# Fewer weight pieces split ahead, the first attention's rotation on VectorE alone, and two state-space operations moved to VectorE

## The chip, the cores and the metric

The kernel runs on one core of one Trainium2 chip. What counts is the device time of one execution in microseconds (us). Each version is timed in several runs; the median is compared.

## The reference, cut to what matters

Two blocks of two layers each, on one sequence of 256 tokens of width 1024, all in float32. The first block has a short convolution mixer, then a dilated-window attention with three groups of eight heads, each layer followed by a squared-ReLU MLP and a gated per-layer projection. The second block has SwiGLU layers around a state-space mixer, and an attention that shares keys and values. The attention of the first block rotates the first 32 of the 128 rows of each query and key head:

```python
def partial_rotary(x, positions):
    ...
    x1 = xf[..., :half]
    x2 = xf[..., half:ROPE_DIM]
    out = jnp.concatenate([x1 * cos - x2 * sin, x2 * cos + x1 * sin, xf[..., ROPE_DIM:]], axis=-1)
```

The state-space mixer is a linear recurrence over the sequence with complex coefficients, written as an associative scan:

```python
    _, _, x_re, x_im = lax.associative_scan(combine, (la_re, la_im, bu_re, bu_im), axis=1)
```

## The kernel before

Activations stay in SBUF, transposed: 128 rows of the width by 256 tokens. Weights come from memory in pieces of 128x2048 float32 values (1 MB), in one fixed order, PLAN. To keep float32 accuracy each weight piece and each activation is split into a rounded part and a rest: ScalarE copies a half piece of 128x1024 into whi (L289), VectorE subtracts it from the raw piece into wlo (L290). Three matmuls then make one product: high by high, high by low, low by high (mm3, L362 to L364). One piece is 48 matmuls.

Three pieces of raw weights, and three of whi and wlo, fit into the ring of buffers. piece() hands out the split piece that is due. On the way it calls fetch(), which splits up to three pieces ahead (ahead=3) and loads up to six ahead. split() is the loop that does so; split_open() takes the buffers, split_half() issues the two instructions for a half piece.

A norm needs the sum of squares of the new activations before its factor R is known. The matmuls of the next phase start without it; its evacuations (rotate, evac, gate) are put on the list "late" by when_scaled() and issued once norm_bc() has made R. In piece(), a fetch that comes in the second piece of such a phase goes on the same list, if two pieces are split ahead:

```python
        if 0 < len(self.todo) < 4 and self.n_split >= i + 2:

            self.late.append(lambda: self.behind(fetch))
        else:
            fetch()
```

behind() ties its instructions to follow the last ones traced on each engine. Background work (tables and weights of the state-space mixer, built during the MLPs; keys and values later) advances by steps, each tied to follow in the same way.

The order on each engine is fixed when the kernel is compiled (TCARGS, L208): a scheduler walks through the program on a modelled time line, gives each engine the earliest instruction in program order that is ready, and lets later work go ahead where an engine would idle. The order of the first attention's pieces is written out by hand (ATT_SEQ, L60). On the chip each engine runs its list in order.

In the first attention, qk() makes one query and one key head of one group in an accumulator, and rotate() scales by R, shuffles the first 32 rows, multiplies by sine and cosine and adds, on POOL (L764 to L767), then splits the result into qh and ql. head() does scores, softmax, transposes and the product with the values. In s5(), chain(q) runs the recurrence of a quarter of the channels: two products, an add, a scan, two products, a difference.

Of the kernel before, what the change touches and what calls it, by code (L numbers as in the profile page):

```python
# [10 lines left out]
F32 = mybir.dt.float32  # L11
# [3 lines left out]
OP = mybir.AluOpType  # L15
# [3 lines left out]
S = 256  # L19
# [113 lines left out]
PLAN = plan()  # L133
# [89 lines left out]
class Ker:  # L223
# [17 lines left out]
    def load(self, i):  # L241
        nc = self.nc
        while self.n_load < min(i, len(PLAN)):
# [22 lines left out]
            self.raw[n] = t  # L266
            self.n_load += 1

    def split(self, i):
        while self.n_split < min(i, len(PLAN)):  # L270
            todo = self.split_open(1)
            for c in range(2):
                self.split_half(todo, c)
# [467 lines left out]
    def attention_(self, x):  # L741
        nc, at = self.nc, self.pp
# [7 lines left out]
        swap = [(i + 16) % 32 for i in range(32)]  # L750
        bc = lambda t: t[:, None, :].to_broadcast([32, 2, S])
        V, QK = {}, {}

        def qk(h, g):
            acc = self.cols(x, "attn_w_qkv", 0, (g * D + h * 128, A + g * D + h * 128),
                            ps="big" if (h, g) == (1, 0) else "acc")
            self.when_scaled(lambda: rotate(h, g, acc))

        def rotate(h, g, acc):
            t = at.tile([128, 2, S], F32, name="qkt")  # L760
            nc.vector.tensor_tensor(t, acc, self.bc2(self.R), op=OP.mult)
            s = at.tile([32, 2, S], F32, name="qks", bufs=1)
            nc.vector.stream_shuffle(s, t[:32], swap)
            nc.gpsimd.tensor_tensor(s, s, bc(self.rS), op=OP.mult)  # L764
            c = at.tile([32, 2, S], F32, name="qkc", bufs=1)
            nc.gpsimd.tensor_tensor(c, t[:32], bc(self.rC), op=OP.mult)  # L766
            nc.gpsimd.tensor_tensor(t[:32], c, s, op=OP.add)  # L767
            qh = at.tile([128, 2, S], F32R, name=f"qh{g}")
            ql = at.tile([128, 2, S], F32R, name=f"ql{g}")
            self.hilo(t, qh, ql)  # L770
            QK[h, g] = qh, ql
# [74 lines left out]
        for hp in range(4):  # L846
            h0 = 2 * hp
            hg = [(h, g) for h in (h0, h0 + 1) for g in range(3)]
            for e in ATT_SEQ.split():
                i = int(e[1])  # L850
# [323 lines left out]
    def s5(self, upd):  # L1174
        nc, bp, tab = self.nc, self.pp, self.s5tab
        v, gp, ac, pe = nc.vector, nc.gpsimd, nc.scalar, nc.tensor
# [3 lines left out]
        for j in range(4):  # L1180
# [6 lines left out]
            s = sq if j == 0 else self.wk.tile([128, 2, S], F32, name="sqt")  # L1187
# [61 lines left out]
        def chain(q):  # L1249
            cs = slice(512 * q, 512 * q + 512)  # L1250
            zs = Zq.pop(q)
            z, zx = self.psum(), self.psum()
            for i in range(4):
                c = slice(128 * i, 128 * i + 128)
                pe.transpose(z[:, c], zs[:, i, :128], self.ident)
                pe.transpose(zx[:, c], zs[:, i, 64:], self.ident)
            Z, Zs, w, ws = (bp.tile([128, 512], F32, name=n) for n in ("sZ", "sZs", "sw", "sws"))
            v.tensor_tensor(Z, z, tab["C"][:, cs], op=OP.mult)
            v.tensor_tensor(Zs, zx, tab["S"][:, cs], op=OP.mult)
            gp.tensor_tensor(Z, Z, Zs, op=OP.add)  # L1260
            v.tensor_tensor_scan(w, tab["D"][:, cs], Z, 0.0, op0=OP.mult, op1=OP.add)
            ac.activation(ws[:64], w[64:], AF.Copy)
            ac.activation(ws[64:], w[:64], AF.Copy)
            (v if q > 1 else gp).tensor_tensor(w, w, tab["C"][:, cs], op=OP.mult)
            v.tensor_tensor(ws, ws, tab["S"][:, cs], op=OP.mult)
            X = Xp[q] = bp.tile([128, 16, 33], F32, name="sX")
            gp.memset(X[:, :, 0:1], 0.0)
            v.tensor_tensor(X[:, :, 1:], w3(w), w3(ws), op=OP.subtract)
# [18 lines left out]
        def presplit(c):  # L1287
            with self.in_order():
                if c == 0:
                    split.extend(self.split_open(3))  # L1290
                self.split_half(split, c)
# [5 lines left out]
        def result(hf):  # L1297
# [9 lines left out]
            for k in range(4 * hf, 4 * hf + 4):  # L1307
                self.hilo(Y[0][:, k], x[0][k], x[1][k])

        steps = {"r": rows_in, "w": wi, "c": chain, "t": to, "o": wo, "R": result,  # L1310
                 "P": lambda: presplit(0), "Q": lambda: presplit(1),
                 "T": lambda: self.table(AF.Gelu_apprx_tanh), "S": lambda: self.table(AF.Sigmoid)}
# [4 lines left out]
        def upd2(j):  # L1317
            if j == 0:
                accs.extend(self.cols_open("s5_w_glu_2", 0, (256 * i, 256 * i + 128), ahead=3 - i) for i in range(3))
                for ks in (range(4), range(4, 8)):  # L1320
                    for a in accs:
                        self.cols_part(x, a, ks)
                self.split(self.n_use + 2)
            elif j == 1:
                a = self.cols_open("s5_w_glu_2", 0, (768, 896))
                self.cols_part(x, a, range(8))
                accs.append(a)
            s = bp.tile([128, 2, S], F32, name="sZ")
            ac.activation(s, accs[j][0], AF.Sigmoid)
            v.tensor_tensor(s, s, Y[0][:, 2 * j:2 * j + 2], op=OP.mult)  # L1330
            v.tensor_tensor(self.h[j], self.h[j], s, op=OP.add)

        self.cap = len(PLAN)
        return self.norm_feed(upd2, ("ffn2_norm_2", 0))


# [562 lines left out]
```

## Time and profile before

| | |
|---|---|
| median of 3 runs | 1887.13 us (1886.97 to 1888.66) |
| profiled execution, its time | 1886.46 us |
| its span, first to last instruction | 1884.7 us |
| mean granted TensorE clock | 0.985 |
| busy: TensorE, VectorE, ScalarE, POOL | 1824.6, 1293.1, 956.5, 466.5 us |

The profile is of one execution. "Busy" is the time in which an engine ran instructions; a wait is the time an engine idled before an instruction, put down to the instruction that released it last. The granted clock is the share of full speed that TensorE was given.

### The profile page before, as it was taken

What the parts mean: (1) busy time and instruction counts of PE and PEld (TensorE: products, weight loads), DVE (VectorE), ACT (ScalarE), POOL (GpSimd) and SP (SyncE); (2) the same over time, 40 slices, a digit from 0 to 9 for tenths busy, and PEclk for the clock granted to TensorE, in tenths of its full rate; (3) what the DMA queues carried; (4) which work ended last, traced back from release to release, by engine and by line L of the source; (5) the groups of instructions that cost most, each with busy time, mean ns of one, the idle gap of its engine ahead of it and who ended that gap; (6) DMA issues with size and microseconds to landing.
All of it is one profiled execution on the core that took longest, in us unless ns stands there. A gap on an engine that the chain in (4) does not pass through costs nothing.

```text
span 1884.7 us, 36094 instructions
## 1 busy us (share of the span) xinstructions
PE 1824.6 (97%) x15242; PEld 1798.8 (95%) x15242; DVE 1293.1 (69%) x1647; ACT 956.5 (51%) x1438; POOL 466.5 (25%) x391
## 2 busy tenths in 40 slices
PE   8999999899999999998999889999999999999999
PEld 8999999899999999998999888999999999899998
DVE  6879987786777788767655585555686556776554
ACT  3455556454455555556444465444565445764442
POOL 2120013555564232211101212110153113421110
PEclk9999999899999999999999989999999999899999
DMA  6565666343343476665555844755455453345452
GB/s 229 203 208 187 220 210 202 140 170 130 147 153 139 172 253 233 216 203 205 202 186 185 294 181 177 246 182 186 163 182 199 175 191 103 56 166 179 179 180 88
DMA packets 80657, 344.72 MB, mean 183 GB/s; under 512 B 8214, under 2 KB 34570, under 8 KB 44656
## 3 DMA queue, kind: packets, MB, share of 16 engines
q1 hardware_dynamic: 79344, 339.33, 51.4%
q0 software_dynamic: 1008, 2.91, 0.5%
q8 instruction: 119, 1.95, 0.4%
q14 instruction: 42, 0.34, 0.1%
q10 hardware_dynamic: 144, 0.20, 0.0%
HBM read 328.73 MB, written 17.86 MB: 184 GB/s over the span
## 4 chain that ended last, share of the span: by engine, by line
PE 76%; DVE 8%; POOL 7%; ACT 4%; issue 3%; DMA 2%; SPq 0%; POOLq 0%; ACTq 0%; DVEq 0%
PE acc L364 15%; PE acc L363 15%; PE acc L362 15%; PE big L364 9%; PE big L363 8%; PE big L362 8%; POOL qkt L767 3%; POOL qks L764 3%; DVE wlo L290 2%; POOL qkc L766 2%; ACT whi L289 1%; PE acc L1724 1%; ACT qh L438 1%; DMA s5wi<-wi 1%; PE misc L513 1%
## 5 line engine op out<-in xcount | busy, mean ns | idle before, releaser
L290 DVE TENSOR_TENSOR wlo<-raw,whi 128x1024 fp32r<-128x1024 f32 x558 | 709.7, 1283 | 312.4 <-ACT whi L289 308.9
L289 ACT ACTIVATE whi<-raw 128x1024 fp32r<-128x1024 f32 x558 | 581.2, 1056 | 538.7 <-PE acc L363 277.2
L362 PE MATMUL acc<-xh,whi 128*128 128x256 f32 x2096 | 597.5, 286 | 10.4 <-ACT xh L441 3.5
L364 PE MATMUL acc<-xh,wlo 128*128 128x256 f32 x2096 | 598.2, 286 | 5.6 <-DVE wlo L439 3.6
L363 PE MATMUL acc<-xl,whi 128*128 128x256 f32 x2096 | 596.6, 285 | 1.6 <-DVE xl L442 1.5
L362 PEld LDWEIGHTS acc<-xh,whi 128*128 128x128 f32 x2096 | 405.4, 194 | 13.2 <-ACT xh L441 3.7
L364 PEld LDWEIGHTS acc<-xh,wlo 128*128 128x128 f32 x2096 | 405.4, 194 | 7.9 <-DVE wlo L439 4.3
L363 PEld LDWEIGHTS acc<-xl,whi 128*128 128x128 f32 x2096 | 405.6, 194 | 2.3 <-DVE xl L442 1.8
L363 PE MATMUL big<-hl,whi 128*128 128x256 f32 x1216 | 344.1, 284 | 0.0
L364 PE MATMUL big<-hh,wlo 128*128 128x256 f32 x1216 | 342.9, 284 | 0.0
L362 PE MATMUL big<-hh,whi 128*128 128x256 f32 x1216 | 342.4, 283 | 0.0
L363 PEld LDWEIGHTS big<-hl,whi 128*128 128x128 f32 x1216 | 232.8, 191 | 1.1 <-issue 1.1
L364 PEld LDWEIGHTS big<-hh,wlo 128*128 128x128 f32 x1216 | 232.0, 191 | 1.5 <-issue 1.5
L362 PEld LDWEIGHTS big<-hh,whi 128*128 128x128 f32 x1216 | 232.2, 191 | 0.2 <-issue 0.2
L887 POOL TENSOR_TENSOR e<-e,R 128x512 f32<-128x512 f32 x44 | 74.0, 1681 | 555.1 <-ACT e L886 545.9
L363 PE MATMUL acc<-yl,whi 128*128 128x256 f32 x720 | 203.1, 284 | 0.6 <-DVE yl L488 0.6
L364 PE MATMUL acc<-yh,wlo 128*128 128x256 f32 x720 | 203.0, 284 | 0.0
L362 PE MATMUL acc<-yh,whi 128*128 128x256 f32 x720 | 202.2, 285 | 0.5 <-ACT yh L474 0.5
L363 PEld LDWEIGHTS acc<-yl,whi 128*128 128x128 f32 x720 | 137.9, 192 | 1.3 <-DVE yl L488 1.3
L362 PEld LDWEIGHTS acc<-yh,whi 128*128 128x128 f32 x720 | 137.4, 193 | 1.2 <-ACT yh L474 0.7
L364 PEld LDWEIGHTS acc<-yh,wlo 128*128 128x128 f32 x720 | 138.0, 192 | 0.1
L482 POOL TENSOR_TENSOR sq<-sq,sqt 128x512 f32<-128x512 f32 x27 | 41.6, 1540 | 138.8 <-ACT sqt L481 138.2
(440 smaller groups left out, 2604.3 us busy)
## 6 DMA issues: line engine op xcount, KB each, us to landing
raw<-in_wst SPq DMA_DIRECT2D x277, 1024.0 KB, 4.9
s5wo<-b SPq DMA_DIRECT2D x8, 512.0 KB, 6.3
s5wi<-wi SPq DMA_DIRECT2D x16, 256.0 KB, 5.4
s5to<-s5k SPq DMA_DIRECT2D x32, 128.0 KB, 4.5
bias<-zb SPq DMA_DIRECT2D x16, 256.0 KB, 4.5
cbt<-zb SPq DMA_DIRECT2D x4, 900.0 KB, 6.2
raw<-s5to SPq DMA_DIRECT2D x6, 512.0 KB, 5.4
raw<-in_wst SPq DMA_DIRECT2D x4, 512.0 KB, 8.1
```

The costliest lines, as they stand in the source:

```text
L289: nc.scalar.activation(hi.t[c], rc, AF.Copy)
L290: nc.vector.tensor_sub(lo.t[c], rc, hi.t[c].bitcast(F32))
L362: mm(out, lh, rh, start=first, stop=False, skip_group_check=True)
L363: mm(out, lh, rl, start=False, stop=False, skip_group_check=True)
L364: mm(out, ll, rh, start=False, stop=last, skip_group_check=True)
L438: nc.scalar.activation(hi, src, AF.Copy)
L482: nc.gpsimd.tensor_tensor(self.sq, self.sq, s, op=OP.add)
L513: self.nc.tensor.matmul(ss[:, t], sq[:, o, 128 * t:128 * t + 128], self.ones[:, :2], start=(i == 0 and t == 0 and o == 0), stop=(o == n - ...
L764: nc.gpsimd.tensor_tensor(s, s, bc(self.rS), op=OP.mult)
L766: nc.gpsimd.tensor_tensor(c, t[:32], bc(self.rC), op=OP.mult)
L767: nc.gpsimd.tensor_tensor(t[:32], c, s, op=OP.add)
L887: nc.gpsimd.tensor_tensor(T[i], T[i], self.bc2(self.R), op=OP.mult)
```

## The change

split() splits at most one piece in a call, where it split as many as were due; the call after the state-space mixer's first three glu pieces asks for one piece less. In the first attention the two rotation tables are multiplied by R once (tables()), the shuffle reads the accumulator, and product and sum run on VectorE; the buffers of the shuffled tile become two. In the state-space chain the add and the product with the cosine table run on VectorE for every quarter. The order of the attention's pieces stays.

```diff
     def split(self, i):
-        while self.n_split < min(i, len(PLAN)):
+        if self.n_split < min(i, len(PLAN)):
             todo = self.split_open(1)
             for c in range(2):
                 self.split_half(todo, c)
@@
+        RS = at.tile([32, S], F32, name="RS", bufs=1)
+
+
+        def tables():
+            nc.vector.tensor_tensor(RS, self.rS, self.R[:32], op=OP.mult)
+            nc.vector.tensor_tensor(self.R[:32], self.rC, self.R[:32], op=OP.mult)
+
+        self.when_scaled(tables)
@@
             nc.vector.tensor_tensor(t, acc, self.bc2(self.R), op=OP.mult)
-            s = at.tile([32, 2, S], F32, name="qks", bufs=1)
-            nc.vector.stream_shuffle(s, t[:32], swap)
-            nc.gpsimd.tensor_tensor(s, s, bc(self.rS), op=OP.mult)
-            c = at.tile([32, 2, S], F32, name="qkc", bufs=1)
-            nc.gpsimd.tensor_tensor(c, t[:32], bc(self.rC), op=OP.mult)
-            nc.gpsimd.tensor_tensor(t[:32], c, s, op=OP.add)
+            s = at.tile([32, 2, S], F32, name="qks")
+            nc.vector.stream_shuffle(s, acc[:32], swap)
+            nc.vector.tensor_tensor(s, s, bc(RS), op=OP.mult)
+            nc.vector.tensor_tensor(t[:32], t[:32], s, op=OP.add)
@@
-            gp.tensor_tensor(Z, Z, Zs, op=OP.add)
+            v.tensor_tensor(Z, Z, Zs, op=OP.add)
@@
-            (v if q > 1 else gp).tensor_tensor(w, w, tab["C"][:, cs], op=OP.mult)
+            v.tensor_tensor(w, w, tab["C"][:, cs], op=OP.mult)
@@
-                self.split(self.n_use + 2)
+                self.split(self.n_use + 1)
```

## Rows read from the trace of the kernel before

**Rows 1.** The page's busy time of each engine: us (share of the span) xinstructions

```profile
PE 1824.6 (97%) x15242; PEld 1798.8 (95%) x15242; DVE 1293.1 (69%) x1647; ACT 956.5 (51%) x1438; POOL 466.5 (25%) x391
```

**Rows 2.** Waits of TensorE, whole span: us in total, times, longest us

```profile
PE big L819 <- ACT p L812: 8.2, 4, 2.8
PE big L362 <- ACT whi L289: 5.7, 3, 3.1
PE big L1232 <- DVE sX L1268: 4.1, 2, 2.6
...
PE acc L362 <- ACT xh L441: 3.5, 1, 3.5
PE acc L362 <- ACT whi L289: 2.7, 2, 2.3
...
PE acc L362 <- DVE e L544: 2.4, 1, 2.4
...
PE big L364 <- DVE wlo L290: 2.0, 1, 2.0
PE acc L364 <- DVE wlo L290: 2.0, 2, 1.0
...
PE acc L363 <- DVE xl L442: 1.5, 1, 1.5
```

**Rows 3.** Windows of 25 us: length, busy us by engine, PEclk, DMA share, GB/s

```profile
325.00:350.00 25.00, 22.22 (x161) 21.71 (x160) 17.61 (x23) 12.21 (x22) 8.49 (x6) 0.86 0.57 208
350.00:375.00 25.00, 19.79 (x149) 19.13 (x147) 19.30 (x21) 11.03 (x14) 18.86 (x10) 0.93 0.33 126
500.00:525.00 25.00, 22.16 (x174) 21.95 (x174) 17.35 (x24) 12.07 (x18) 15.16 (x9) 0.93 0.35 129
850.00:875.00 25.00, 19.98 (x147) 19.48 (x146) 23.66 (x33) 19.59 (x39) 1.68 (x1) 0.86 0.54 196
1075.00:1100.00 25.00, 15.87 (x261) 12.89 (x250) 23.25 (x28) 13.47 (x27) 7.30 (x7) 0.73 0.48 190
1125.00:1150.00 25.00, 21.73 (x168) 21.26 (x167) 13.74 (x18) 12.69 (x19) 8.29 (x14) 0.93 0.24 87
1325.00:1350.00 25.00, 22.43 (x171) 21.93 (x170) 15.54 (x20) 10.80 (x18) 5.79 (x8) 0.93 0.36 127
```

**Rows 4.** Windows while a norm's R is outstanding, columns (PE, PEld, DVE, ACT, POOL) as above

```profile
842.20:849.00 6.80, 6.80 (x58) 6.75 (x57) 0.48 (x2) 0.20 (x1) 1.32 (x2) 1.00 0.12 49
...
1331.30:1339.00 7.70, 7.64 (x63) 7.38 (x61) 0.16 (x1) 0.26 (x1) 2.48 (x4) 1.00 0.17 60
```

**Rows 5.** Timeline of ScalarE around 849 and 1339 us: start, us, instruction

```profile
849.08 4.84 ACT L289 ACTIVATE whi<-raw 128x1024 fp32r<-128x1024 f32 x5
853.82 1.14 ACT L704 ACTIVATE e<-e 128x512 f32<-128x512 f32 x2
...
1339.02 4.84 ACT L289 ACTIVATE whi<-raw 128x1024 fp32r<-128x1024 f32 x5
```

**Rows 6.** Groups of instructions, 350 to 600 us: xcount | busy, mean ns | idle before

```profile
L766 POOL TENSOR_TENSOR qkc<-qkt,rC 32x512 f32<-32x512 f32 x24 | 53.4, 2223 | 26.4 <-DVE qkt L761 25.7
L764 POOL TENSOR_TENSOR qks<-qks,rS 32x512 f32<-32x512 f32 x24 | 48.1, 2004 | 7.0 <-DVE qks L763 7.0
...
L290 DVE TENSOR_TENSOR wlo<-raw,whi 128x1024 fp32r<-128x1024 f32 x71 | 99.9, 1416 | 8.4 <-ACT whi L289 8.2
L439 DVE TENSOR_TENSOR ql<-qkt,qh 128x512 fp32r<-128x512 f32 x24 | 23.5, 981 | 46.2 <-ACT qh L438 46.2
```

**Rows 7.** Groups of instructions, 1055 to 1100 us, and (last) 1700 to 1880 us

```profile
L1260 POOL TENSOR_TENSOR sZ<-sZ,sZs 128x512 f32<-128x512 f32 x4 | 5.5, 1379 | 11.3 <-DVE sZs L1259 11.3
...
L1259 DVE TENSOR_TENSOR sZs<-acc,tS 128x512 f32<-128x512 f32 x4 | 2.7, 673 | 0.0
...
L290 DVE TENSOR_TENSOR wlo<-raw,whi 128x1024 fp32r<-128x1024 f32 x60 | 73.5, 1228 | 58.4 <-ACT whi L289 58.4
```

**Rows 8.** Windows of 25 us in the convolution and the first MLP

```profile
50.00:75.00 25.00, 25.00 (x210) 25.00 (x210) 24.84 (x35) 12.23 (x15) 3.51 (x2) 1.00 0.67 253
...
175.00:200.00 25.00, 25.00 (x211) 25.00 (x210) 24.15 (x47) 13.14 (x18) 0.00 (x0) 1.00 0.60 208
```

## Prediction

> **What bounds the kernel now.** I read the page first: TensorE is busy 97% of a 1884.7 us span [rows 1], so everything else can gain only through the 3% in which TensorE idles and through time at its lower clock. The second view is the list of TensorE's waits [rows 2]: the reader should see that few lines carry it, and that most name the split of a weight piece (whi on ScalarE, L289; wlo on VectorE, L290), or what stands queued behind splits. The third is the span in slices of 25 us [rows 3]: seven of them have a granted clock under 1.00, and each holds some of those waits. So a wait costs twice: its idle time, and the part of the slice at half rate (1.2 instead of 2.4 GHz). A clock of 0.86 over 25 us is 0.14 x 25 = 3.5 us lost, 0.93 is 1.75 us.
>
> Then I asked why splits are late. Just before the late ones, VectorE and ScalarE do nothing: between 1331.3 and 1339.0 us they are busy 0.16 and 0.26 us, between 842.2 and 849.0 us 0.48 and 0.20 us [rows 4]. Straight after, ScalarE runs five halves in one go, from 1339.02 and from 849.08 us, and at 849 the sigmoid (L704) waits behind them till 853.82 [rows 5]. That is the hold in piece(): while the norm's broadcast R is outstanding, the second piece's fetch goes on the late list and is issued behind R and the first evacuation. The engines idle, then have everything to do at once.
>
> **The change, part by part.**
>
> *Splitting.* In the loop as it is, the call for piece i splits i+2 (first_feed leaves n_split at 1, piece 0 splits two). With one per call (one whole piece: both its halves still follow) it splits i+1, and never catches up, since each call also uses one. The state-space stage opens three pieces ahead; the glu's call, now n_use + 1, brings it back to one ahead; after the second attention (cap) the call for piece i splits i itself. The number of split instructions and DMAs does not change: 558 halves either way. Nor does the buffer that a split waits for: three pieces of whi and wlo. What changes is the place in program order, and the schedule is made ahead of time from program order by a scheduler that also takes ready work early. So where VectorE has room, I cost the move at nothing: a split still starts when its buffer is free. Two things do follow.
>
> First, on entry n_split is i+1, so the test n_split >= i+2 in piece() fails and the hold is never used. The splits held today can run in the idle stretches of [rows 4], where 7.7 and 6.8 us are free and a piece needs 2 x 1.23 us on VectorE [rows 7]. Place by place, idle time [rows 2] plus clock [rows 3]; lower bound nothing everywhere, since a shorter wait may only move to the next buffer:
> - near 330 us (projection behind the first MLP): 2.4 + 3.5 = 5.9. The wait is for an evacuation (e, L544) that stands behind splits, and one split fewer goes ahead of it; I take 3.
> - near 354 us (attention begins): 3.1 + 2.0 + 1.75 = 6.85. This split is held behind the first rotation too; I take 5.5.
> - near 858 us: 3.5 + 1.5 + 3.5 = 8.5. VectorE is busy 23.66 of 25 us there, so some stays; I take 5.
> - near 884 us: 0.4 + 1.0 = 1.4; I take 1.
> - near 1141 us: 2.3 + 1.0 + 1.75 = 5.05; I take 4.
> - near 1339 us: 2.6 + 1.75 = 4.35; I take 3.5.
> Together at most 32.05, taken 22.
>
> Second, in stretches where VectorE is full (24.84 of 25 us from 50, 24.15 from 175 [rows 8]), evacuations and background work now rank ahead of a split that they used to follow. What covers this is one piece of TensorE work, 48 matmuls at about 210 to a 25 us slice [rows 8], 5.7 us, where the two-ahead order had two. Without the cover each late split costs as at 1141 us, 3.3 us idle, or 5.05 with the clock. I take one such place in full, 5 us lost; bounds none and the rival below.
>
> *Rotation.* Removed are three POOL operations in each of 24 rotations: qkc (L766) at 2.22 us, and qks and qkt at 2.0 each (two more lines like it), 6.2 us in a row [rows 6]. Added are two 32x512 operations on VectorE. No VectorE row has that form; a 128x512 one takes 0.67 [rows 7], and a row with nothing to do is the floor, so 0 to 0.67 each, and I take 0.67, as elements per partition are the same. The two tables are one-off, two 32x256 operations, under 1.4 us behind R. The chain from accumulator to rotated tile shrinks by 6.2 - 1.3 = 4.9 us. The shuffle now reads the accumulator, which stays taken one shuffle longer; with three accumulators I cost that at nothing. VectorE gains 48 x 0.67 = 32 us and loses the stretching beside POOL: 71 wlo at 1416 instead of 1228 ns, 13.3 us, and 24 ql at 981 instead of some 670, 7.5 us [rows 6, 7]. Net 11 us more over 250 us, on an engine at 19.3 and 17.35 of 25 us [rows 3], so it stays under 85% and off the path.
>
> What that is worth is read from TensorE: VectorE is in order, and its ql instructions sit 46.2 us waiting for POOL's chain through qh [rows 6]; the softmax queued behind gets late, and the transposes wait 8.2 us for p [rows 2]. With the slice at 500 us (1.75) the bound is 9.95 us; below, nothing. I take 7.5, since the softmax also comes ahead of one more split.
>
> The Trainium skill (GPSIMD Engine Reference, Key points) has VectorE about 2x faster for elementwise work. The rows here give 2.22 against 0.67, or 3.3x. By the page's ratio a rotation's chain would lose 3 x 1.34 - 1.34 = 2.7 us, and the 7.5 would scale to about 4 (an estimate), so 1863 in place of 1860.
>
> *State-space operations.* Four adds (L1260) leave POOL at 1.38 us for 0.67 on VectorE, 2.8 us off the four chains; two products move likewise, but ran beside VectorE's own. The added six are 4.1 us on an engine at 23.25 of 25 us there [rows 3, 7], which is the lower bound (a loss of 4.1); the upper is the 2.8 plus stalls beside POOL, about 4.5. TensorE waits 4.1 us there for the chain's result sX [rows 2]. I take a gain of 2.5, nearer to the chain.
>
> **Sum.** 22 + 7.5 + 2.5 - 5 = 27 us off the profiled execution's 1886.46 gives 1859.5; the median of the runs is 0.7 above that execution, so 1860.
>
> **The rivals.**
> - *The hold was not the cause*: the buffers, which come free only as TensorE finishes a piece, keep the splits late anyway. For it: a split must wait for the piece three before it. Against it: both engines idle for 7 us and start the moment R is there [rows 4, 5]. Then only 7.5 + 2.5 - 5 = 5 remain: 1882.
> - *Late splits in full stretches* (the other side): from 125 to 250 us, where the background tables are built and VectorE is nearly full [rows 8], there are some 22 pieces, plus the twelve of the convolution. If lumps of background work exceed the cover of one piece, each late split costs 3.3 to 5.05. Against 32 of gains, seven to ten late ones cancel it; fifteen at 5 give 1886.5 - 32 + 75 = 1929, ten at 4 about 1895. For it: 24 of 25 us busy. Against it: no single stretch waits today, the order between engines is still greedy, and the work does not grow.
> - *VectorE becomes attention's bound*: the added 32 us are not paid back, and the splits there slip. Then the 7.5 turn to a loss of the same size: 1875.
>
> **How the numbers follow.** Forecast 0.68, hold not the cause 0.10, late splits 0.15, VectorE in attention 0.07. A measurement of this kernel can tell about 0.2%, 3.8 us, from no change. Faster: 0.68 + 0.07, and a third of the rival at 1882, which sits near that line, with the smaller late-split cases the other way: 0.75. Same: 0.09. Slower: 0.16. With every bound gained the time is 1886.5 - 46.5 = 1840; I put the low end at 1842. The likeliest alone would lie within 1842 to 1876; the range goes up to 1890 to take in the rivals, leaving out the worse half of late splits and little below.
>
> **What would show it.** Right: at the six places ScalarE and VectorE split while R is outstanding; the waits of acc and big for whi and wlo fall from 12.4 us to a few; slices at 850, 1125 and 1325 us come back to 1.00; POOL is nearly empty from 350 to 600 us, ql no longer idles for qh, wlo there takes about 1.23 us, and the waits for p go. Wrong: new waits for whi or wlo between 50 and 250 us or after the second attention, clock dips where there are none today, or the same bursts behind R.

## The result, and the profile after

The changed kernel takes 1845.91 us (median of 4 runs, 1844.06 to 1846.42); the kernel before, beside it, takes 1887.05. The ratio is 0.9778, 95% interval 0.9761 to 0.9795: 41 us faster. The forecast was 1860 us, in a range of 1842 to 1890. So the direction was right and the time is in the range, but the gain is half as large again as the 27 us that were summed up.

The page of the kernel after, its busy line [rows 1] and its chain that ended last (share of the span by engine):

```profile
PE 1812.6 (98%) x15242; PEld 1790.1 (97%) x15242; DVE 1302.7 (71%) x1703; ACT 964.5 (52%) x1438; POOL 304.8 (17%) x313
...
PE 93%; DVE 2%; issue 2%; ACT 1%; DMA 1%; POOL 0%; SPq 0%; DVEq 0%; ACTq 0%
```

The span went from 1884.7 to 1844.3 us, TensorE's idle time fell by 28.4 us (60.1 to 31.7), and its busy time by 12.0 although it runs the same 15242 instructions: that part is the clock. POOL lost 162 us of work, VectorE gained 10.

The waits of TensorE after, as in [rows 2] (us in total, times, longest us):

```profile
PE big L1239 <- issue: 6.4, 3, 3.6
PE acc L365 <- DVE wlo L440: 3.8, 2, 2.6
PE acc L363 <- ACT e L893: 3.1, 1, 3.1
PE acc L363 <- DVE e L654: 2.3, 1, 2.3
```

No wait names a weight split (whi, now L290, or wlo, now L291) any more, and none names the softmax p; together these were 20.6 us in [rows 2]. (wlo of L440 is another tile, from the first 15 us.) What leads the list now is the state-space stage (L1239), and two waits for an evacuation e, at 857 us (L893) and at 619 us (L654). Both are new: at these pieces of work the kernel before lost 0.4 and 1.0 us to a split (near 884 us) and nothing.

The windows of 25 us [rows 3], at the same clock times, though the work comes up to 40 us earlier now (length, busy us by engine, clock, DMA share, GB/s):

```profile
350.00:375.00 25.00, 25.00 (x211) 25.00 (x210) 23.55 (x37) 11.52 (x14) 0.00 (x0) 1.00 0.55 194
500.00:525.00 25.00, 25.00 (x213) 25.00 (x212) 18.94 (x30) 14.19 (x24) 0.69 (x1) 1.00 0.41 156
600.00:625.00 25.00, 22.56 (x173) 22.13 (x172) 23.57 (x27) 12.95 (x18) 13.71 (x10) 0.93 0.51 189
825.00:850.00 25.00, 25.00 (x209) 24.82 (x208) 22.52 (x33) 19.96 (x38) 2.15 (x1) 1.00 0.55 195
850.00:875.00 25.00, 21.85 (x168) 21.43 (x168) 17.78 (x27) 11.78 (x16) 6.42 (x6) 0.93 0.65 260
1050.00:1075.00 25.00, 17.65 (x209) 15.27 (x201) 21.23 (x32) 15.99 (x30) 0.26 (x2) 0.66 0.30 119
1125.00:1150.00 25.00, 25.00 (x203) 24.02 (x203) 15.13 (x15) 11.85 (x15) 1.75 (x2) 1.00 0.64 222
1325.00:1350.00 25.00, 25.00 (x206) 24.52 (x205) 21.72 (x21) 15.58 (x20) 13.69 (x13) 1.00 0.47 169
50.00:75.00 25.00, 25.00 (x211) 25.00 (x210) 21.84 (x35) 11.30 (x15) 2.58 (x2) 1.00 0.56 202
175.00:200.00 25.00, 25.00 (x211) 25.00 (x210) 22.64 (x40) 14.25 (x18) 0.00 (x0) 1.00 0.57 208
```

The dips at 350, 500, 1125 and 1325 us are gone, and so is that of [rows 3] at 850, whose work now runs from 825 at full clock. The two dips at 600 and 850 us are those of the two new waits, and the state-space stage (1050) has 0.66 over its worst slice. The last two rows answer to [rows 8]: no late split there, the rival of the other side did not come.

The timeline of ScalarE of the kernel after, around the two norms whose splits were bunched in [rows 5] (start, us, instruction):

```profile
819.13 1.06 ACT L290 ACTIVATE whi<-raw 128x1024 fp32r<-128x1024 f32 x1 [3.57 <-PE acc L364]
821.89 1.06 ACT L290 ACTIVATE whi<-raw 128x1024 fp32r<-128x1024 f32 x1 [1.70 <-PE acc L364]
823.04 0.38 ACT L540 ACTIVATE R<-misc 128x256 f32<-128x256 f32 x1
...
1299.21 1.06 ACT L290 ACTIVATE whi<-raw 128x1024 fp32r<-128x1024 f32 x1 [2.50 <-PE acc L364]
1301.42 2.01 ACT L290 ACTIVATE whi<-raw 128x1024 fp32r<-128x1024 f32 x2 [1.15 <-PE acc L364]
1305.13 1.06 ACT L290 ACTIVATE whi<-raw 128x1024 fp32r<-128x1024 f32 x1 [1.71 <-PE acc L364]
1306.29 0.38 ACT L540 ACTIVATE R<-misc 128x256 f32<-128x256 f32 x1
```

Before, five halves came in one go behind R. Now two and four halves are copied ahead of R, and where ScalarE idled ahead of one, the name in the brackets is a matmul of TensorE: the split runs as soon as its buffer is free.

The groups of VectorE in the first attention, 345 to 600 us, as in [rows 6] (xcount | busy, mean ns | idle before):

```profile
L291 DVE TENSOR_TENSOR wlo<-raw,whi 128x1024 fp32r<-128x1024 f32 x74 | 89.7, 1213 | 26.1 <-ACT whi L290 25.6
L772 DVE STREAM_SHUFFLE qks<-acc 32x512 f32<-32x512 f32 x23 | 16.8, 731 | 0.0
L440 DVE TENSOR_TENSOR ql<-qkt,qh 128x512 fp32r<-128x512 f32 x24 | 16.2, 679 | 0.0
L774 DVE TENSOR_TENSOR qkt<-qkt,qks 32x512 f32<-32x512 f32 x24 | 16.1, 673 | 0.2
L773 DVE TENSOR_TENSOR qks<-qks,RS 32x512 f32<-32x512 f32 x24 | 16.1, 672 | 0.0
```

The two new operations take 0.67 us each, as taken; ql no longer idles (46.2 us before) and fell from 981 to 679 ns, wlo from 1416 to 1213.

**Where the 40 us of the span went.** TensorE runs the same 15242 instructions in all these kernels, and outside the state-space stage in an order that hardly differs, so the time from the start of its n-th instruction to that of its m-th can be compared. Worked out so from the traces (us; the columns on the right are the first two experiments):

| instructions of TensorE | starts before at | before | after | splitting alone | rotation alone | the forecast took |
|---|---|---|---|---|---|---|
| 2000 to 2400, background tables | 252 | 48.2 | 46.2 | 46.2 | 48.1 | - |
| 2400 to 2800, places at 330 and 354 | 300 | 60.7 | 48.2 | 48.2 | 59.9 | -8.5 |
| 2800 to 4800, first attention | 360 | 252.2 | 237.8 | 251.9 | 239.6 | -7.5 |
| 4800 to 5200, second MLP begins | 613 | 48.3 | 51.9 | 50.4 | 48.2 | +5, late splits anywhere |
| 6800 to 7000, place at 858 | 849 | 31.6 | 24.3 | 24.3 | 32.0 | -5 |
| 7000 to 7200, place at 884 | 881 | 26.3 | 29.0 | 28.9 | 27.3 | -1 |
| 8400 to 9200, state-space stage | 1051 | 79.1 | 80.8 | 82.2 | 80.3 | -2.5 |
| 9200 to 9600, place at 1141 | 1130 | 54.0 | 49.4 | 49.0 | 52.5 | -4 |
| 9600 to 11200, place at 1339 | 1184 | 197.4 | 192.7 | 192.7 | 197.4 | -3.5 |
| 12800 to 13200, second attention | 1573 | 60.0 | 57.5 | 57.5 | 60.6 | - |

The rows add up to 40.0 us less; all else together differs by 0.3. Two traces of one kernel differ too: the first 2000 instructions took 250.8 us here and 248.9 in a second trace of the changed kernel, and instructions 4800 to 5200 took 51.9 and 50.3.

### The profile page after: what moved, and what is told of

Same layout as the page of the kernel before. It is cut to its first block, busy times and chain, and to the rows that moved or that the text cites. A ratio compares the mean times of both kernels' runs of the same rounds, so it can differ in the third digit from the quotient of the medians.

```text
span 1844.3 us, 36052 instructions
## 1 busy us (share of the span) xinstructions
PE 1812.6 (98%) x15242; PEld 1790.1 (97%) x15242; DVE 1302.7 (71%) x1703; ACT 964.5 (52%) x1438; POOL 304.8 (17%) x313
## 4 chain that ended last, share of the span: by engine, by line
PE 93%; DVE 2%; issue 2%; ACT 1%; DMA 1%; POOL 0%; SPq 0%; DVEq 0%; ACTq 0%
PE acc L363 19%; PE acc L364 19%; PE acc L365 19%; PE big L365 10%; PE big L364 10%; PE big L363 10%; PE acc L1731 1%; PE big L1711 1%; PE misc L514 1%; DVE wlo L291 0%; PE big L1239 0%; PE big L1669 0%; PE misc L1474 0%; DMA h<-in_xT 0%; PE misc L1126 0%
## 5 line engine op out<-in xcount | busy, mean ns | idle before, releaser
L291 DVE TENSOR_TENSOR wlo<-raw,whi 128x1024 fp32r<-128x1024 f32 x558 | 702.4, 1264 | 362.9 <-ACT whi L290 361.4
L290 ACT ACTIVATE whi<-raw 128x1024 fp32r<-128x1024 f32 x558 | 587.2, 1058 | 666.7 <-PE acc L364 380.2
```

The lines of the kernel that those rows point to most:

```text
L290: nc.scalar.activation(hi.t[c], rc, AF.Copy)
L291: nc.vector.tensor_sub(lo.t[c], rc, hi.t[c].bitcast(F32))
```

## The experiments

All ran with the kernel before beside them (medians of 1885.18 to 1886.15 us in four jobs). Kernels of one job are compared with each other first.

**Splitting alone.** The kernel before, with the two hunks of splitting:

```diff
-        while self.n_split < min(i, len(PLAN)):
+        if self.n_split < min(i, len(PLAN)):
...
-                self.split(self.n_use + 2)
+                self.split(self.n_use + 1)
```

Expected: 

> The kernel before with the split change alone (one piece per call, and the glu's call asking for one less); rotation and state-space operations stay on POOL. Theory (the unused hold carries the gain at the norms): the time lost near 330, 354, 858, 1141 and 1339 us comes back, some 25 us, and the attention's body from 360 to 610 us keeps its waits for p: 1860 us. Rival (the rotation on POOL is what kept the attention's start and body back): about 17 us come back, 1870 us, and the wait for whi near 354 us stays. Rival (one piece ahead makes late splits, which the rotation's change hid): 1885 us or more.

Measured: 1860.93 us (1859.04 to 1863.70), ratio 0.9876 (0.9858 to 0.9894), 24.5 us off. Each norm place takes what it takes after the change (table), and the softmax waits stay. From the waits of TensorE of this kernel:

```profile
PE big L819 <- ACT p L812: 8.5, 4, 2.8
...
PE acc L362 <- ACT e L886: 3.1, 1, 3.1
PE acc L362 <- DVE e L653: 2.3, 1, 2.3
```

Both new waits for e are here already, so they belong to the splitting.

**Rotation alone.** The kernel before, with the rotation and its tables as in the change:

```diff
+            nc.vector.tensor_tensor(RS, self.rS, self.R[:32], op=OP.mult)
+            nc.vector.tensor_tensor(self.R[:32], self.rC, self.R[:32], op=OP.mult)
...
-            nc.gpsimd.tensor_tensor(s, s, bc(self.rS), op=OP.mult)
...
-            nc.gpsimd.tensor_tensor(t[:32], c, s, op=OP.add)
...
+            nc.vector.stream_shuffle(s, acc[:32], swap)
+            nc.vector.tensor_tensor(s, s, bc(RS), op=OP.mult)
+            nc.vector.tensor_tensor(t[:32], t[:32], s, op=OP.add)
```

Expected: 

> The kernel before with the rotation change alone. Theory (POOL's chain blocks VectorE, which blocks the softmax): the waits for p go, the attention from its 400 matmul steps near 360 to 610 us gains 10 to 14 us, and at its start at most the 2 us by which the held split no longer stands behind POOL: 1873 us. Rival (the attention's gain came from the softmax ranking ahead of one more split): 3 us or less, 1884 us. The norms near 858, 1141 and 1339 us keep their bursts and waits.

Measured: 1873.88 us (1872.53 to 1875.16), ratio 0.9944 (0.9928 to 0.9959), 11.6 us off. The attention lost 12.6 us (table) and the waits for p are gone, while the waits for splits at the norms are all there:

```profile
PE big L362 <- ACT whi L289: 6.3, 3, 3.7
PE acc L362 <- ACT whi L289: 3.8, 3, 1.9
```

**The hold taken out, nothing else.** The kernel before, still splitting as many as are due:

```diff
-        if 0 < len(self.todo) < 4 and self.n_split >= i + 2:
-
-            self.late.append(lambda: self.behind(fetch))
-        else:
-            fetch()
+        fetch()
```

Expected: 

> The kernel before with the hold alone taken out: each fetch is issued at once, the loop still splits all that is due, two ahead. Theory (the hold is the cause): VectorE and ScalarE split while R is outstanding and the norms' places come back, 20 to 25 us: 1864 us. Rival (it is the place in program order, one piece ahead instead of two, that lets evacuations go first): at most a third of it, 1880 us, with evacuations late near 330 and 858 us. Rival (the buffers decide): no change, 1887 us.

Measured: 1861.72 us (1859.61 to 1862.77), ratio 0.9875 (0.9857 to 0.9894). That is the gain of splitting alone, 0.8 us apart with overlapping runs. So the hold was the cause, and the edit to split() works because it leaves the hold unused, not because it splits less. The new wait for e behind the second MLP is here too (29.2 us from instruction 7000 to 7200), but not the one at 619 us (49.1 from 4800 to 5200): that one comes with one piece per call.

**The hold brought back.** The changed kernel, with the test fitted to one piece ahead:

```diff
-        if 0 < len(self.todo) < 4 and self.n_split >= i + 2:
+        if 0 < len(self.todo) < 4 and self.n_split >= i + 1:
```

Expected: 

> The changed kernel with the hold brought back into use (its test asks for one piece ahead instead of two); all else as changed. Theory (the hold is the cause): at each norm the third piece's split now waits for R, so the waits for whi near 345, 850, 1110 and 1305 us return, some 4 us a place or more, 1865 us or above. Rival (program order, not the hold): within 4 us of the changed kernel, 1846 to 1850 us.

Measured: 1893.53 us (1892.45 to 1899.42), ratio 1.0052 (1.0035 to 1.0070). From its waits of TensorE:

```profile
PE acc L363 <- ACT whi L290: 23.0, 8, 7.4
...
PE acc L365 <- DVE wlo L291: 5.5, 8, 1.0
```

The waits for splits are back, and larger than before: 47.6 us lost against the changed kernel (1845.91, in another job). It costs more than the hold of the kernel before gave back: 16 to 18 us of it fall into the first 2000 instructions (266.6 us against 250.8 and 248.9), where the kernel before lost nothing to it (250.5 us with its hold, 250.4 without). That with one piece ahead TensorE has one piece less to live on while a split is held would explain the size; it wasn't tried apart. This and the run before it settle the first rival (1882 us) from both sides.

**The changed kernel again,** as the base of the three that follow. Expected: 

> The changed kernel once more, beside the three that follow: 1846 us, within 2 us, and the same wait of 2.3 us for an evacuation (e) near 619 us.

Measured: 1843.65 us (1843.18 to 1847.00), ratio 0.9782 (0.9769 to 0.9795). That is just more than 2 us under the 1846 expected; the wait of 2.3 us is there again.

**State-space operations back on POOL.** The changed kernel with

```diff
-            v.tensor_tensor(Z, Z, Zs, op=OP.add)
+            gp.tensor_tensor(Z, Z, Zs, op=OP.add)
...
-            v.tensor_tensor(w, w, tab["C"][:, cs], op=OP.mult)
+            (v if q > 1 else gp).tensor_tensor(w, w, tab["C"][:, cs], op=OP.mult)
```

Expected: 

> The changed kernel with the two state-space operations back on POOL. If moving them gains what the prediction took (2.5 us), this is 1848.5 us. Rival: the lower bound holds, VectorE at 23 of 25 us only gets more to do, and the move loses up to 4.1: 1842 to 1845. Third: the chain is hidden, 1846.

Measured: 1844.80 us (1842.27 to 1845.87), ratio 0.9779 (0.9766 to 0.9792): no difference that can be told. The number itself lies in the band of the second case, but the kernel beside it came out at 1843.65 and not at 1846, so the move is worth nothing here, the third case.

**Two pieces ahead again, without the hold.** The changed kernel with

```diff
-        if self.n_split < min(i, len(PLAN)):
+        while self.n_split < min(i, len(PLAN)):
...
-        if 0 < len(self.todo) < 4 and self.n_split >= i + 2:
-
-            self.late.append(lambda: self.behind(fetch))
-        else:
-            fetch()
+        fetch()
...
-                self.split(self.n_use + 1)
+                self.split(self.n_use + 2)
```

Expected: 

> The changed kernel, but split as many pieces as are due, two ahead, with the hold in piece() taken out. Theory: the whole gain of the splitting edit comes from the hold that is no longer used, and the number of pieces ahead is worth nothing: 1846 us, within 2. Rival: with the rotation on VectorE too, one piece less ahead of each evacuation is worth 3 us or more: 1849 to 1855, with new waits for p or e.

Measured: 1840.89 us (1840.22 to 1841.84), ratio 0.9760 (0.9747 to 0.9774), 2.8 us faster than the changed kernel beside it, with no overlap of the runs. Both expectations missed: splitting one at a time is not worth nothing, and not a gain, but a small loss. Two stretches carry it. Instructions 4800 to 5200 take 49.0 us instead of 50.3, since the wait for e at 619 us is gone, and the state-space stage, 8400 to 9200, takes 77.4 instead of 80.9. Some of it goes again elsewhere: instructions 2000 to 2800 take 1.2 us more, as they do with the hold alone taken out.

**Background work of the second MLP later.** The changed kernel with

```diff
-            self.background(self.s5_weights((1, 2, 3)), rate=R1)
+            self.background(self.s5_weights((1, 2, 3)), rate=R1, delay=2)
```

What stands behind the wait at 619 us is in the timelines of VectorE and, below it, POOL of the kernel after:

```profile
614.80 2.38 DVE L1093 TENSOR_TENSOR bba<-bba,btt 128x256 f32<-128x256 f32 x1
617.10 1.21 DVE L291 TENSOR_TENSOR wlo<-raw,whi 128x1024 fp32r<-128x1024 f32 x1
618.23 2.15 DVE L1095 TENSOR_TENSOR btt<-zi,bcm 128x256 f32<-128x256 f32 x1
620.30 1.28 DVE L654 SCALAR_TENSOR_TENSOR e<-acc,R 128x512 f32<-128x512 f32 x2
621.50 0.41 DVE L1096 TENSOR_TENSOR bbb<-bbb,btt 128x256 f32<-128x256 f32 x1
```

```profile
614.69 2.21 POOL L1133 TENSOR_TENSOR b<-tE,bcm 128x1152 f32<-128x1152 f32 x1
617.25 2.84 POOL L1137 TENSOR_TENSOR b<-tE,bba 128x1024 f32<-128x1024 f32 x1 [0.36 <-DVE bba L1093]
```

R is there at 615.3 us, but the first evacuation starts at 620.3: two background operations and a split stand ahead of it in VectorE's list. A background operation of this shape takes 0.41 us when POOL is quiet (621.50), and the two ahead of the evacuation take 2.38 and 2.15; each ends 0.3 us behind POOL's operation beside it (616.90 and 620.09).

Expected: 

> The changed kernel, with the background work of the second MLP begun two steps later, so that VectorE meets the first evacuation before it. Theory: the wait near 619 us (2.3 us idle, 3.4 us at half clock, 4.0 in all) was that background work ahead of the evacuation, and goes: 1842 us. Rival: the work, pushed back, comes in the way of the next evacuations or of the end of the second MLP near 857 us: 1846 or more.

Measured: 1839.10 us (1837.52 to 1839.78), ratio 0.9749 (0.9736 to 0.9763), and in a second run, below, 1837.23. So 4.6 us faster than the changed kernel beside it, about as expected, but not where it was expected: instructions 4800 to 5200 gained only 0.5 us (49.8 against 50.3 in the changed kernel's second trace, whose wait cost less clock than in the first; a new wait of 1.1 us for xl stands at 598.6), and 6800 to 7200 gained 4.5 (48.9 against 53.4). The wait for e behind the second MLP went from 3.15 to 0.47 us and its dip with it. The window at that place in this kernel:

```profile
850.00:875.00 25.00, 24.53 (x203) 24.28 (x202) 20.14 (x26) 12.37 (x16) 6.85 (x5) 1.00 0.62 229
```

In the changed kernel's second trace a whi (852.74 us) goes ahead of the copy of R (853.70) on ScalarE, and a wlo (853.82) ahead of the first e (854.97) on VectorE. In this one R (850.33) and both e (850.75 and 851.36) go ahead of that split (851.64 and 852.73). So the order fixed at compile time came out better there. The edit lies some 240 us earlier in the program; by which step of the scheduler it reached this place is open.

**Both of these together.** The changed kernel with the last two edits. Expected: 

> Both edits that gained beside the changed kernel: two pieces ahead without the hold, and the later background work of the second MLP. If their gains are of different waits they add up: 1836 us. Rival: both only moved the same first evacuations ahead of the same background work, so the second adds nothing: 1839 to 1841.

Measured: 1839.92 us (1839.25 to 1840.48), ratio 0.9758 (0.9744 to 0.9771). The gains don't add, and the number is the rival's, but not for its reason. The state-space stage is short again (76.0 us), but the wait for e of 3.1 us behind the second MLP is back (29.2 us from instruction 7000 to 7200, 25.0 with the later background work alone).

**The later background work again,** in the same job. Expected: 

> The changed kernel with the later background work once more, beside the run with both edits: 1839 us, within 2 us; TensorE's wait for an evacuation near 857 us stays under 1 us, as in its first run (0.47).

Measured: 1837.23 us (1836.76 to 1837.64), ratio 0.9743 (0.9730 to 0.9757): as expected, with the wait at 0.47 us again; it is the fastest kernel of the study, 2.7 us ahead of both edits together.

**One piece per call, two ahead only from the glu on.** The kernel with the later background work, and

```diff
-        if 0 < len(self.todo) < 4 and self.n_split >= i + 2:
...
+        fetch()
...
-                self.split(self.n_use + 1)
+                self.split(self.n_use + 2)
```

Expected: 

> The changed kernel with the later background work, one piece per call, but the call after the first three glu pieces asks for one piece more again (two ahead from there on), and the hold taken out. Both runs with two pieces ahead passed the state-space stage in 125.4 and 126.3 us where those with one took 128.8 to 130.3 (from the 8400th to the 9600th instruction of TensorE). Theory: that call is the reason, and the stage takes about 126 here too: 1834 us. Rival: the shorter stage came from elsewhere (where the half-clock stretches fall): 129 to 130 there, 1838 us.

Measured: 1837.93 us (1836.78 to 1838.51), ratio 0.9751 (0.9737 to 0.9764); the state-space stage, 8400 to 9600, takes 130.0 us. The theory fell: that call is not what makes the stage longer.

**Two ahead, state-space operations on POOL.** The kernel with two pieces ahead and no hold, with the operations moved back as in the diff further up. Expected: 

> Two pieces ahead, no hold, rotation on VectorE, but the two state-space operations on POOL as before: beside the run with two ahead (1841 us) it is their price where the splits keep their distance. If they gain there what that stage hints (126.3 us against 129.9 with the operations on POOL): 1844.5 us. Rival: their move is worth nothing, as with one piece ahead: 1841 us.

Measured: 1844.97 us (1842.85 to 1847.13), ratio 0.9789 (0.9776 to 0.9803), 4.1 us slower than with them on VectorE (in another job, against its own runs of before; the runs don't overlap), and 129.8 us for the stage against 126.4. So the same two operations are worth 4 us here and nothing in the changed kernel.

Where the difference lies, the windows of this stage show: the changed kernel (second trace), the changed kernel with the operations on POOL, two ahead, two ahead with the operations on POOL, and two ahead with the later background work (columns as in the windows further up):

```profile
1017.20:1098.10 80.90, 69.77 (x802) 65.29 (x802) 59.29 (x84) 46.33 (x76) 7.40 (x10) 0.89 0.61 223
1017.20:1097.90 80.70, 68.09 (x802) 63.06 (x801) 59.83 (x78) 46.27 (x76) 17.32 (x16) 0.92 0.62 228
1019.40:1096.80 77.40, 66.70 (x802) 62.66 (x801) 60.58 (x85) 47.83 (x79) 8.33 (x14) 0.93 0.67 245
1019.20:1100.00 80.80, 66.99 (x802) 62.42 (x801) 59.90 (x78) 46.20 (x76) 17.30 (x16) 0.94 0.63 229
1018.50:1094.50 76.00, 66.08 (x803) 62.05 (x802) 59.52 (x85) 47.27 (x77) 7.45 (x10) 0.93 0.68 245
```

TensorE's idle time is the length less its busy time. With the operations on VectorE it idles less both times: 11.1 us against 12.6 with one piece per call, 10.7 against 13.8 with two ahead. With two ahead the clock is nearly the same and the gain stays. With one piece per call the granted clock is lower (0.89 against 0.92), the same matmuls keep TensorE busy 1.7 us longer, and the gain is gone. Between the changed kernel and two ahead, too, idle time differs by 0.4 us and busy time by 3.1: nearly all of the 3.5 us is the clock.

An order of ScalarE's suggests itself as the cause. In the changed kernel the copy ush stands ahead of the last quarter's sws (first two rows), the last quarter's result sX comes late by it, and TensorE waits 3.16 us for it; with two ahead sws goes first (1056.43, ush at 1060.58) and the wait is 0.35. But with two ahead and the later background work ush goes first as well (last two rows), and that stage is the shortest of all:

```profile
1057.17 1.12 ACT L1207 ACTIVATE ush<-big 128x512 f32<-128x512 f32 x1 [2.06 <-PE big L1310]
1058.31 0.63 ACT L1269 ACTIVATE sws<-sw 64x512 f32<-64x512 f32 x1
...
1055.15 1.08 ACT L1203 ACTIVATE ush<-big 128x512 f32<-128x512 f32 x1 [1.99 <-PE big L1306]
1056.26 0.63 ACT L1265 ACTIVATE sws<-sw 64x512 f32<-64x512 f32 x1
```

So this order alone doesn't set the stage's length. What sets the clock there is open, but it isn't the glu's call. In four further traces with one piece per call and the operations on VectorE it lies between 0.87 and 0.91, and the stage between 79.4 and 80.8 us.

## Why the prediction was right, and where its sizes were off

**Splitting, the hold.** Right, and shown from both sides: taking the hold out of the kernel before gives the gain, bringing it back in the changed kernel loses it. The term was 22 us. The table has 12.5 at the places at 330 and 354 us, 7.3 at 858, 4.6 at 1141 and 4.7 at 1339, 29.1 together where 21 was taken, less 2.7 lost at 884. It was too small above all at the first two and at 858: the bounds, 12.75 and 8.5, were paid nearly in full, and at 1339 the 4.7 is even above the bound of 4.35. Shares had been taken because a shorter wait may move to the next buffer, because evacuations stand behind splits (330) and because VectorE is busy (858). Little was lost to any of these: the splits still wait for their buffers (the brackets above), but no wait of TensorE names a split any more.

**Late splits in full stretches.** Taken as 5 us lost; there is none, neither at 50 nor from 125 to 250 us. What came instead are two late evacuations with R just there: at the start of the second MLP, 2.0 to 3.6 us (three traces), behind background work and a split, and at its end, the 2.7 us at 884, behind a split. The prediction had evacuations move ahead of splits; at these two a split stands ahead of them.

**Rotation.** The chain and the durations were right (0.67 us for a 32x512 product, ql and wlo back at their quiet times). VectorE became busier by 10 us, where 11 was forecast: for instructions 2800 to 4800 it is busy 201.09 us after and 191.35 before, the two rows below (first before, then after; columns as in the windows above).

```profile
360.40:612.60 252.20, 242.19 (x2001) 240.75 (x2001) 191.35 (x262) 125.55 (x196) 146.06 (x75) 0.99 0.41 151
```

```profile
346.20:584.00 237.80, 237.80 (x2003) 237.80 (x2002) 201.09 (x315) 129.50 (x196) 6.66 (x8) 1.00 0.43 155
```

That is 84.6% of the stretch, just under the 85% forecast, and the rival that VectorE becomes the bound (1875 us) did not come: TensorE is busy for all 237.8 us. The value was mis-sized: taken 7.5, measured 14.4 in the whole change and 12.6 by itself. The step that failed is the bound of 9.95 us. It counted only the waits that name p (8.2) and the one clock dip in a row shown. The first of the two rows just above has 252.20 - 242.19 = 10.0 us of idle, waits for the values' vl among it, and the same matmuls kept TensorE busy 4.4 us longer, at a clock of 0.99, than at full clock. Idle time and clock of the whole stage are the 14.4; the waits with one name are not. With the rotation alone the 10.0 us of idle are gone and 1.8 us of the clock remain.

The sentences on the Trainium skill (GPSIMD Engine Reference, Key points) gave 1863 by its ratio of about 2. The means of the product qks, 2004 ns on POOL and 672 on VectorE, have 3.0, but POOL's mean holds waits beside VectorE. The kernel before shows it in two of POOL's operations in a row:

```profile
428.18 4.35 POOL L766 TENSOR_TENSOR qkc<-qkt,rC 32x512 f32<-32x512 f32 x1 [2.13 <-DVE qkt L761]
432.50 1.28 POOL L764 TENSOR_TENSOR qks<-qks,rS 32x512 f32<-32x512 f32 x1
```

Two splits on VectorE (428.71 and 430.18) lie inside the first; beside the second VectorE did nothing. Six of the 24 qks products ran like that, each in 1.28 or 1.29 us, 1.9 times 672 ns. So the page's ratio agrees with operations that nothing disturbs, and the estimate of 1863 left out the waits between the two engines.

**State-space operations.** Taken as a gain of 2.5 us. In the changed kernel they gain nothing that can be told (1.1 us between two medians whose runs overlap, 1.4 in the stage from splitting alone to the whole change), and 4.1 us where two pieces are ahead. The chain did get shorter both times, as TensorE's idle time shows (1.5 and 3.1 us less in the windows of the stage); what the term left out is the stage's clock. Against before, the stage even lost 1.7 us: it idles 10.7 us instead of 12.3, but at a clock of 0.87 instead of 0.91 the same matmuls take 3.3 us longer.

**What was not in the sum.** 2.0 us among the background tables, which comes with the splitting, and 2.5 in the second attention, where a dip is gone. The prediction spoke of seven slices under full clock; the trace of before has others, among them this one, at 0.80:

```profile
1600.00:1625.00 25.00, 23.05 (x137) 20.75 (x138) 19.17 (x53) 18.10 (x67) 11.86 (x25) 0.80 0.36 62
```

It comes and goes between kernels (the stretch takes 60.2 us with the hold alone taken out, 57.5 with splitting alone), and no run isolates its cause.

**The sum, by measured terms:** 29.1 - 2.7 + 14.4 + 2.0 + 2.5 - 1.7 - 3.6 = 40.0, against 22 + 7.5 + 2.5 - 5 = 27 forecast.

## What to carry to other kernels

Where an engine idles for several microseconds and then runs a burst, look in the program for the rule that holds the work back, and try the kernel without it before changing how much is done ahead. Bound what a stage can gain by all idle time and all clock lost in it, not by the waits that carry one name. And in a kernel whose order is fixed at compile time, every edit reshuffles places far away by 2 to 5 us each: judge an edit worth that little beside a second base, since its value hangs on the order that the rest happens to get.

## What the runs showed of the hardware

A VectorE operation on 128x256 values, 0.41 us by itself, took 2.38 and 2.15 us beside POOL operations of 2.21 and 2.84 us, and ended 0.3 us behind them both times, while a split that had begun just ahead of POOL's second operation (617.10 and 617.25) took its usual 1.21. So one of the two waits for the other to end, rather than both running slower. In the kernel after, 30 of the 35 splits that began while POOL ran a product or an add ended 1.08 to 1.09 us behind it, nearly their whole 1.21. It can be POOL that waits: in the two rows of POOL further up its product took 4.35 us while two splits ran, in 1.20 us each. The Trainium skill (SBUF — State Buffer, section "SBUF: two separate sides") states it as an exclusive lock for the whole instruction; these rows agree that one engine waits for all of the other's operation. It makes background work on POOL dear for all that VectorE has queued behind its own next operation.

The shuffle of 32x512 values took 731 ns from the accumulator (L772 above) and 732 from SBUF, as the group in the first attention of splitting alone shows, so reading the accumulator directly cost nothing:

```profile
L763 DVE STREAM_SHUFFLE qks<-qkt 32x512 f32<-32x512 f32 x24 | 17.6, 732 | 0.0
```
